# A two-block transformer kernel on one core: prepared weights, conditioning rows and normed inputs are given out to the engines at other places

## The chip, the core and the metric

The kernel runs on one core of a Trainium2 chip. The core has a matrix engine (PE, which also loads weights: PEld), a vector engine (DVE), an activation engine (ACT), a general engine (POOL) and SyncE (SP), whose queue issues the DMAs. Each engine takes its own instructions strictly in program order and waits for others through semaphores. The metric is the device time of one execution in microseconds, less is better. A difference of 0.2% (about 4 us) is what repeated measurements of this kernel can tell from none.

## The reference

There are 1024 tokens of width 1024, in fp32. A first block mixes (a short and a 31-tap convolution) and has a gated FFN; a second part has one layer with a causal mean pool and one of sliding-window attention, both conditioned by a vector `c`. Cut to what the change touches:

```
g = dwconv(h @ w_gate, conv_ffn_w);  v = h @ w_up
x = x + (silu(g) * v) @ w_down

shift, scale, gate = split(silu(c) @ ada_w[l] + ada_b[l], 3)     # l = 0, 1; the same for kv_ada
h = rmsnorm(rmsnorm(x, norm_final_g), norm_g[0]) * (1 + scale) + shift
u, z = split(h @ a_w_in, 2)
y = (grouped(pool(u), a_w_group) * a_scale * silu(z)) @ a_w_out
x = x + gate * y
k, v = split((rmsnorm(x) * kv_norm_g ... + shift_kv) @ w_kv)
x = x + gate * (attention(h1, k, v) * silu(z)) @ b_w_out;  return rmsnorm(x)
```

## The kernel before, in words

Activations lie transposed, 128 features by 512 tokens in a tile (`c` = 0 or 1 is the half of the tokens). Each fp32 operand is cut in two parts of a shorter format, `hi` (a copy, on ACT) and `lo` (the difference, on POOL or DVE), and each product is three matmuls of 512 columns: hi*hi, lo*hi, hi*lo. The order of every engine's work is the order of the calls in the source (`manual_schedule`); nothing is moved by a planner.

The stages, by time in the profiled execution: input projection and convolutions (0 to 250 us), `w_out` (255 to 344), FFN gate and up products (344 to 776), `w_down` (776 to 1040), the pooled layer's input products (1040 to 1379), its grouped products and output (1379 to 1658), keys and values (1658 to 1690), attention (1690 to 1975), the end (to 2058).

**Products by pairs.** FFN and pooled input products are done for pairs of weight columns and pairs of token halves by seven products instead of eight (class `Pair`, `Products.run`). One step is one product: 12 matmuls. Four of the seven need sums or differences of raw weight halves (`ws`, made by DVE). For each step `prep_to` makes the weights of the step `PREP_AHEAD` = 4 later in one call: `added` on DVE (`ws`), `ACT.copy` to `whi`, and `wlo` on POOL, or on DVE for two of seven. `lead` does the same during the rows of `w_out`, by a table.

**Chains.** Work beside the products is written as generators. `pump` steps each of them once, once per row or step (twice in part of the FFN), and takes a piece from the queue `bg`. `ada_all` is such a chain: for 64 row blocks of the conditioning weights it loads a tile `adaw` (128x1024, 512 KB) and adds it, times a scalar, to two accumulators on DVE, 8 blocks to each of 8 sections, and then sums over partitions. `chain_pool` makes the normed input of the pooled layer from the column sums of squares: `bsum` on DVE, `sums` on PE, a power on POOL, a diagonal on DVE and ACT (`dh`, `dl`), `spread` on PE, then scaled blocks. At its end it makes `R1` by another `diag(power(m))` and `spread`. `WAIT` and bare `yield`s set how many steps lie between these parts.

**Buffers.** `S` takes one of `NS` = 92 slots of 128x512 in turn, `L` one of 8 wide tiles (128x1060) for the convolution's tiles, `adaw`, and in the pooled layer `up` and the running sums `ps`. A tile that takes a used slot waits until its last reader is done, a store to memory (`pp<-ps`) being a reader.

**Pooled output.** `load_group` loads the pooled rows of a group (`pl`) and splits them (`cut`: `ahi` on ACT, `alo` on POOL). `do_gm(g, todo)` does a group's products, each followed by `sz` (DVE) and its split, and takes four pieces of `todo` per row; for the first group `todo` holds loads and 16 times `scale_x` (DVE). `out2` does the output products. `attn` chains then make the normed input (`make_h`: `hu`, `hlo` on DVE); `finish` runs a chain to its end at once.

Of the kernel before, what the change touches and what calls it, by code (L numbers as in the profile page):

```python
# [30 lines left out]
        "ffn0": (2, 1, 1), "ffn1": (4, 1, 3), "pool0": (2, 1, 1), "pool1": (5, 1, 3),  # L31
# [32 lines left out]
def kernel(ctx: ExitStack, tc: tile.TileContext, a: dict, out: bass.AP):  # L64
# [3 lines left out]
    NS = 92  # L68
# [8 lines left out]
    wide = wide_ctx.enter_context(tc.tile_pool(name="wide", bufs=8))  # L77
# [760 lines left out]
    class Pair:  # L838
# [12 lines left out]
        def keep(self, x):  # L851
            hi, lo = S("whi", F32R), S("wlo", F32R)
            ACT.copy(hi, x)  # L853
            small_op["n"] += 1
            eng = DVE if not small_op["early"] and small_op["n"] % 7 in SUB_DVE else POOL
            eng.tensor_tensor(lo, x, r32(hi), ALU.subtract)  # L856
            return hi, lo

# [13 lines left out]
        def prep(self, p):  # L872
# [17 lines left out]
            self.w[p] = self.keep(t)  # L890
# [111 lines left out]
    class Products:  # L1002


        def __init__(self, stage, put):
            self.pairs, self.steps = stage
            self.group = {g: Pair(*g, put(*g)) for g in self.pairs}
            self.ready = 0

        def prep_to(self, n):  # L1010
            while self.ready < min(n, len(self.steps)):
                g, p = self.steps[self.ready]
                self.group[g].prep(p)
                self.ready += 1

        def lead(self, row):

            small_op["early"] = True
            n = row - SUMS_FROM
            if 0 <= n < 2 * SIDE:  # L1020
# [27 lines left out]
    for c in range(NC):  # L1048
        finish(ln[c])
        acc = S("ss")  # L1050
        for d in range(NK):
# [6 lines left out]
            sq_into(acc, x, d == 0)  # L1058
# [12 lines left out]
    def ada_section(i):  # L1071
        kind, l, s = sections[i]
        h = {}
        halves = (slice(0, CH), slice(CH, D))

        def one(k):
            t = L("adaw")
            src = a["ada_w_2"][l] if kind == "ada" else a["kv_ada_w_2"]
            nc.sync.dma_start(out=t[:, 0:D], in_=src[k * 128:(k + 1) * 128, s * D:(s + 1) * D])
            h[k] = t  # L1080

        def mac(k):
            t = h.pop(k)
            if k == 0:
                h["acc"] = P("ada"), P("ada")
            for n, hs in enumerate(halves):
                src = h["acc"][n]
                if k == 0:
                    DVE.tensor_scalar(src, t[:, hs], cact[:, 0:1], None, ALU.mult)
                    continue  # L1090
                dst = src
                if k == 7:
                    dst = h["sum", n] = S("adas")
# [932 lines left out]
```

## Time and profile before

| | |
|---|---|
| median of 3 executions | 2061.04 us (2061.02 to 2062.11) |
| profiled execution | 2060.43 us |
| its span in the trace | 2058.7 us |
| mean granted PE clock | 0.982 |
| PE busy | 1960.1 us (95%) |
| DVE / ACT / POOL busy | 1498.2 / 840.2 / 1011.3 us |

The span goes from the first to the last instruction of the trace; 1.7 us of the execution lie around it. PE matmuls are pipelined, so their busy times overlap; an engine's waits are the idle time before an instruction, with the instruction that released it.

### The profile page before, as it was taken

What the parts mean: (1) busy time and instruction counts of PE and PEld (TensorE: products, weight loads), DVE (VectorE), ACT (ScalarE), POOL (GpSimd) and SP (SyncE); (2) the same over time, 40 slices, a digit from 0 to 9 for tenths busy, and PEclk for the clock granted to TensorE, in tenths of its full rate; (3) what the DMA queues carried; (4) which work ended last, traced back from release to release, by engine and by line L of the source; (5) the groups of instructions that cost most, each with busy time, mean ns of one, the idle gap of its engine ahead of it and who ended that gap; (6) DMA issues with size and microseconds to landing.
All of it is one profiled execution on the core that took longest, in us unless ns stands there. A gap on an engine that the chain in (4) does not pass through costs nothing. (4 is left out here: it accounts for less than half of the span.)

```text
span 2058.7 us, 26114 instructions
## 1 busy us (share of the span) xinstructions
PE 1960.1 (95%) x8920; PEld 1620.7 (79%) x8920; DVE 1498.2 (73%) x2339; ACT 840.2 (41%) x1647; POOL 1011.3 (49%) x851
## 2 busy tenths in 40 slices
PE   7999998999999999999889999988999989999997
PEld 6888876787877878888667788866888778888886
DVE  7899778889978986343776766758444687787866
ACT  6333344433333343211355233233213357778723
POOL 4767465754534468642456343365426353224422
PEclk9999999999999999999989999999999999999999
DMA  6111412045989468532201343256332032111302
GB/s 211 52 62 41 144 62 72 8 143 169 179 156 187 143 217 306 198 122 78 77 31 42 123 129 102 87 208 237 123 120 76 11 123 65 54 57 32 113 1 82
DMA packets 116709, 228.61 MB, mean 111 GB/s; under 512 B 13232, under 2 KB 19808, under 8 KB 116576
## 3 DMA queue, kind: packets, MB, share of 16 engines
q1 hardware_dynamic: 116576, 226.95, 34.9%
q8 instruction: 70, 1.15, 0.2%
q14 instruction: 63, 0.52, 0.1%
HBM read 177.62 MB, written 48.23 MB: 110 GB/s over the span
## 5 line engine op out<-in xcount | busy, mean ns | idle before, releaser
L903 PE MATMUL p<-hhi,whi 128*128 128x512 f32 x1064 | 420.3, 395 | 19.4 <-ACT p L912 11.0
L903 PE MATMUL p<-hhi,wlo 128*128 128x512 f32 x1064 | 418.1, 393 | 8.5 <-POOL wlo L856 8.0
L903 PE MATMUL p<-hlo,whi 128*128 128x512 f32 x1064 | 417.4, 392 | 0.0
L195 POOL TENSOR_TENSOR wlo<-raw,whi 128x512 fp32r<-128x512 f32 x196 | 260.3, 1352 | 183.8 <-ACT whi L194 113.1
L310 PE MATMUL p<-ahi,whi 128*128 128x512 f32 x784 | 312.0, 398 | 5.4 <-DVE sz L1433 3.2
L310 PE MATMUL p<-alo,whi 128*128 128x512 f32 x784 | 310.7, 396 | 1.5 <-POOL alo L421 1.3
L310 PE MATMUL p<-ahi,wlo 128*128 128x512 f32 x784 | 310.3, 396 | 0.0
L856 POOL TENSOR_TENSOR wlo<-ws,whi 128x512 fp32r<-128x512 f32 x116 | 166.7, 1440 | 250.0 <-ACT whi L853 215.7
L903 PEld LDWEIGHTS p<-hhi,whi 128*128 128x128 f32 x1064 | 201.7, 190 | 66.6 <-ACT p L912 13.7
L903 PEld LDWEIGHTS p<-hhi,wlo 128*128 128x128 f32 x1064 | 201.8, 190 | 54.5 <-POOL wlo L856 11.1
L903 PEld LDWEIGHTS p<-hlo,whi 128*128 128x128 f32 x1064 | 202.1, 190 | 41.7
L853 ACT CAST whi<-ws 128x512 fp32r<-128x512 f32 x152 | 92.8, 620 | 270.7 <-DVE ws L861 253.3
L301 PE MATMUL p<-hhi,whi 128*128 128x512 f32 x496 | 196.1, 395 | 6.6 <-ACT hhi L414 6.6
L301 PE MATMUL p<-hlo,whi 128*128 128x512 f32 x496 | 195.6, 394 | 3.3 <-DVE hlo L415 3.3
L301 PE MATMUL p<-hhi,wlo 128*128 128x512 f32 x496 | 195.0, 393 | 0.0
L310 PEld LDWEIGHTS p<-ahi,whi 128*128 128x128 f32 x784 | 150.4, 192 | 38.7 <-DVE sz L1433 4.1
L856 POOL TENSOR_TENSOR wlo<-raw,whi 128x512 fp32r<-128x512 f32 x84 | 120.5, 1440 | 117.8 <-ACT whi L853 109.0
L310 PEld LDWEIGHTS p<-alo,whi 128*128 128x128 f32 x784 | 150.6, 192 | 33.7 <-POOL alo L421 1.6
L310 PEld LDWEIGHTS p<-ahi,wlo 128*128 128x128 f32 x784 | 150.3, 192 | 31.8
L194 ACT CAST whi<-raw 128x512 fp32r<-128x512 f32 x196 | 112.1, 617 | 113.7 <-PE p L310 75.8
L528 DVE SCALAR_TENSOR_TENSOR cps<-u,vec,cps 128x1024 f32<-128x1024 f32 (+1 forms) x140 | 150.6, 1075 | 4.5
L1439 DVE SCALAR_TENSOR_TENSOR x<-p,modv,x 128x512 f32<-128x512 f32 x128 | 94.6, 749 | 67.2 <-PE p L310 66.8
(288 smaller groups left out, 3709.8 us busy)
## 6 DMA issues: line engine op xcount, KB each, us to landing
adaw<-in_ada_w SPq DMA_DIRECT2D x48, 512.0 KB, 6.1
raw<-in_a_w_in SPq DMA_DIRECT2D x64, 256.0 KB, 4.2
raw<-in_w_gate SPq DMA_DIRECT2D x44, 256.0 KB, 5.3
raw<-in_w_up SPq DMA_DIRECT2D x44, 256.0 KB, 6.0
ff<-f SPq DMA_DIRECT2D x44, 256.0 KB, 2.8
raw<-in_w_down SPq DMA_DIRECT2D x44, 256.0 KB, 5.1
fl<-ff SPq DMA_DIRECT2D x44, 256.0 KB, 5.4
raw<-in_w_in SPq DMA_DIRECT2D x40, 256.0 KB, 3.1
```

The source lines that it names most:

```text
L194: (DVE.tensor_copy if on_dve else ACT.copy)(hi, t)
L195: (DVE if on_dve else POOL).tensor_tensor(lo, t, r32(hi), ALU.subtract)
L301: PE.matmul(ps, lhsT=wt[k // 4][:, sl], rhs=hh[k, c], start=(n == 0), stop=(n == 23))
L310: PE.matmul(ps, lhsT=wt[d // 4][:, sl], rhs=hh[c], start=(n == 0), stop=(n == last))
L528: DVE.scalar_tensor_tensor(dst[:, lo:hi], u[:, lo + k:hi + k], V("conv_b_w", k * 4 + j), src[:, lo:hi], ALU.mult, ALU.add)
L853: ACT.copy(hi, x)
L856: eng.tensor_tensor(lo, x, r32(hi), ALU.subtract)
L903: PE.matmul(ps, lhsT=wt[:, sl], rhs=hh, start=(begins and n == 0), stop=(n == 11), skip_group_check=True)
L1439: DVE.scalar_tensor_tensor(X[d, c], ps, modv[:, goff + d:goff + d + 1], X[d, c], ALU.mult, ALU.add)
```

## The change

- `prep_to` gives the weights out in three calls: at a step, the `lo` on DVE of the product prepared a call before, then `whi` and the POOL `lo`, and last the source (`ws` or the raw half) of the product after it. `PREP_AHEAD` is 5. The table of `lead` and the rows in which sums are made are new.
- `ada_all` loads the conditioning rows in two halves of 256 KB into general slots, two row blocks ahead across sections; it starts 6 steps later; a section's last sums are a chain of their own. `NS` is 96, and there are 6 wide tiles instead of 8; the pool `qp` of attention's `qa`, `qb` is gone (they take slots).
- The squares of the first half of `w_out` are added on POOL.
- `sums` of the pooled input's first half comes one row later; `R1` 24 and 8 `yield`s later instead of 1 and 3.
- The first group's cuts come one at a step, from one step earlier on, the odd ones on DVE. `do_gm(0)` takes two pieces of `todo` per row and splits `sz` on POOL; half of `scale_x` is left to `out2`.
- In attention's first chain 4 `yield`s come before `make_h`, and the chain is run to its end after the key and value products, not ahead of them.

```
-        "ffn0": (2, 1, 1), ... "pool0": (2, 1, 1), ...
+        "ffn0": (2, 1, 1), ... "pool0": (3, 1, 1), ...
-PREP_AHEAD = 4
-FFN_DMA = 120
-LEAD = (2, 4, 5, 6, 6, 6, 7, 8)
-SUMS_FROM = 3
+PREP_AHEAD = 5
+FFN_DMA = 126
+LEAD = (3, 5, 6, 6, 7, 7, 8, 8)
+SUMS_ROWS = (0, 1, 2, 3, 4, 5, 6, 11)
+ADA_AHEAD = 2
-    NS = 92
+    NS = 96
-    wide = wide_ctx.enter_context(tc.tile_pool(name="wide", bufs=8))
+    wide = wide_ctx.enter_context(tc.tile_pool(name="wide", bufs=6))
...
         def prep_to(self, n):
+            for f in [self.queue.pop(0) for _ in range(len(self.queue))]:
+                f()
             while self.ready < min(n, len(self.steps)):
                 g, p = self.steps[self.ready]
-                self.group[g].prep(p)
+                self.queue.append(lambda p=p, pair=self.group[g], x=self.group[g].source(p): self.high(pair, p, x))
                 self.ready += 1
+        def high(self, pair, p, x):
+            hi, lo = S("whi", F32R), S("wlo", F32R)
+            ACT.copy(hi, x)
+            pair.w[p] = hi, lo
+            small_op["n"] += 1
+            if small_op["early"] or small_op["n"] % 7 not in SUB_DVE:
+                POOL.tensor_tensor(lo, x, r32(hi), ALU.subtract)
+            else:
+                self.queue.append(lambda: DVE.tensor_tensor(lo, x, r32(hi), ALU.subtract))
...
-            sq_into(acc, x, d == 0)
+            sq_into(acc, x, d == 0, None, POOL if c == 0 else None)
...
+    def ada_load(n):
+        ...
+        for h in range(2):
+            t = S("adaw")
+            nc.sync.dma_start(out=t, in_=src[k * 128:(k + 1) * 128, s * D + h * CH:s * D + (h + 1) * CH])
+            ada_w[n].append(t)
...
     def ada_all():
-        for i in range(8):
-            yield from ada_section(i)
+        for n in range(ADA_AHEAD):
+            ada_load(n)
+            yield
+        for n in range(8 * len(sections)):
+            ada_load(n + ADA_AHEAD)
+            for _ in range(ADA_GAP):
+                yield
+            ...
+            yield
+            if k == 7:
+                launch(ada_fin(n // 8, h))
...
-        if n == 2 * EARLY + 5 * SIDE:
+        if n == 2 * EARLY + 5 * SIDE + 6:
             chains.append(ada_all())
...
         yield from blocks_of_h(c, get, shift)
-        yield
+        for _ in range(24):
+            yield
         d1 = diag(power(m), POOL)
-        for _ in range(3):
+        for _ in range(8):
             yield
...
-            PP_H[g, k, c], PP_L[g, k, c] = split(tiles.pop((k, c)))
+            PP_H[g, k, c], PP_L[g, k, c] = split(tiles.pop((k, c)), DVE if g == 0 and k % 2 else None)
...
-                    put_act(("m", i), c, split(t, DVE if c else None))
-                    for _ in range(min(4, len(todo))):
+                    put_act(("m", i), c, split(t, DVE if c and g else None))
+                    for _ in range(min(per, len(todo))):
...
-        if left <= 8:
-            for f in nxt["cut"][:2]:
+        if left <= 9:
+            for f in nxt["cut"][:1]:
...
-    do_gm(0, todo)
+    do_gm(0, todo, 2)
     for g in range(3):
         todo = [f for part_ in load_group(g + 1) for f in part_]
-        out2(g, 0, todo, 2 if g == 2 else 1)
+        if g == 0:
+            todo = scales[8:] + todo
+        out2(g, 0, todo, 1 if g == 1 else 2)
...
-        yield
+        for _ in range(4 if c == 0 else 1):
+            yield
         yield from make_h(c, t, 8, MOD_SH1, *SPREAD[f"attn{c}"])
...
-    finish(pend[0])
     for c in range(NC):
         ...
         vt[c] = evac_v(c, kvps[1, c])
+    finish(pend[0])
     finish(pend[1])
```

Where the instructions now stand is told at three places. The first is DVE in the FFN, a few steps of one pair (`ws` a weight sum, `wlo` a low part, `c`, `f` and `g` the gate's convolution and the products' sums). Before:

```order
L968 TENSOR_TENSOR g<-p,p_4396 128x512
L856 TENSOR_TENSOR wlo<-raw,whi 128x512
L942 SCALAR_TENSOR_TENSOR c_4650<-g,vec,c_4650 128x1024
L996 TENSOR_TENSOR f<-p,p_4421 128x512
L861 TENSOR_TENSOR ws<-raw 128x512
L861 TENSOR_TENSOR ws<-ws,raw 128x512
L942 SCALAR_TENSOR_TENSOR c_4650<-g,vec,c_4650 128x1024
L968 TENSOR_TENSOR g<-p,q 128x512
L861 TENSOR_TENSOR ws<-raw 128x512
L861 TENSOR_TENSOR ws<-ws,raw 128x512
L856 TENSOR_TENSOR wlo<-ws,whi 128x512
```

And now:

```order
L990 TENSOR_TENSOR f<-p,p_4431 128x512
L1021 TENSOR_TENSOR wlo<-raw,whi 128x512
L854 TENSOR_TENSOR ws<-raw 128x512
L854 TENSOR_TENSOR ws<-ws,raw 128x512
L936 SCALAR_TENSOR_TENSOR c_4667<-g,vec,c_4667 128x1024
L962 TENSOR_TENSOR g<-p,q 128x512
L1131 SCALAR_TENSOR_TENSOR ada<-adaw,cact,ada 128x512 x2
L978 TENSOR_TENSOR f<-f,c_4667 128x512
L990 TENSOR_TENSOR f<-p,q 128x512
L1021 TENSOR_TENSOR wlo<-ws,whi 128x512
L936 SCALAR_TENSOR_TENSOR c_4722<-g,vec,c_4722 128x1024
```

The two weight sums stand at the same place among the products' sums or one ahead, and the `wlo` of a sum, which followed it at once, now has a step's other work ahead of it, half a block of conditioning among it.

The second place is POOL near the end of the pooled input products, where the pooled rows of the first group are cut (`alo<-pl`) between the weights (`wlo`). Before:

```order
L856 TENSOR_TENSOR wlo<-ws,whi 128x512
L421 TENSOR_TENSOR alo<-pl,ahi 128x512 x2
L856 TENSOR_TENSOR wlo<-raw,whi 128x512
L421 TENSOR_TENSOR alo<-pl,ahi 128x512 x2
L856 TENSOR_TENSOR wlo<-ws,whi 128x512
L195 TENSOR_TENSOR wlo<-raw,whi 128x512 x2
L1340 MEMSET up 128x16
L421 TENSOR_TENSOR alo<-pl,ahi 128x512 x2
L856 TENSOR_TENSOR wlo<-ws,whi 128x512
```

And now:

```order
L1019 TENSOR_TENSOR wlo<-ws,whi 128x512
L422 TENSOR_TENSOR alo<-pl,ahi 128x512
L1019 TENSOR_TENSOR wlo<-raw,whi 128x512
L422 TENSOR_TENSOR alo<-pl,ahi 128x512
L1019 TENSOR_TENSOR wlo<-ws,whi 128x512
L196 TENSOR_TENSOR wlo<-raw,whi 128x512 x2
L1355 MEMSET up 128x16
L1019 TENSOR_TENSOR wlo<-ws,whi 128x512
L422 TENSOR_TENSOR alo<-pl,ahi 128x512
```

Between two weights there stands one cut where there were two, and the last `wlo` shown has no cut between it and the pair of group weights ahead of it.

The third place is DVE where the pooled block ends (`hu`, `hlo` of the attention's input, half 0; `tr`, `bsum` the column sums of the squares of half 1; `r` what follows from them). Before:

```order
L1285 SCALAR_TENSOR_TENSOR hu<-x,gain,R 128x512
L1279 SCALAR_TENSOR_TENSOR hlo<-hu,modv,hhi 128x512
L1285 SCALAR_TENSOR_TENSOR hu<-x,gain,R 128x512
L1279 SCALAR_TENSOR_TENSOR hlo<-hu,modv,hhi 128x512
L1525 COPY kvb<-sums 32x1 x4
L1439 SCALAR_TENSOR_TENSOR x<-p,modv,x 128x512
L415 SCALAR_TENSOR_TENSOR hlo<-x,gain,hhi 128x512 x2
L338 STREAM_TRANSPOSE tr<-ssa 128x512
L339 TENSOR_REDUCE bsum<-tr 128x16
L361 TENSOR_SCALAR r<-sums 32x4 x4
L371 CAST rh<-q 128x4
L372 TENSOR_TENSOR rl<-q,rh 128x4
```

And now:

```order
L416 SCALAR_TENSOR_TENSOR hlo<-x,gain,hhi 128x512 x2
L339 STREAM_TRANSPOSE tr<-ssa 128x512
L340 TENSOR_REDUCE bsum<-tr 128x16
L1299 SCALAR_TENSOR_TENSOR hu<-x,gain,R 128x512 x2
L1293 SCALAR_TENSOR_TENSOR hlo<-hu,modv,hhi 128x512
L1299 SCALAR_TENSOR_TENSOR hu<-x,gain,R 128x512
L1293 SCALAR_TENSOR_TENSOR hlo<-hu,modv,hhi 128x512
L1299 SCALAR_TENSOR_TENSOR hu<-x,gain,R 128x512 x2
L1293 SCALAR_TENSOR_TENSOR hlo<-hu,modv,hhi 128x512
L1299 SCALAR_TENSOR_TENSOR hu<-x,gain,R 128x512
L1293 SCALAR_TENSOR_TENSOR hlo<-hu,modv,hhi 128x512
L362 TENSOR_SCALAR r<-sums 32x4 x4
```

The column sums, which stood behind all `hu` and `hlo` of half 0, now stand ahead of ten of these instructions, and `r` stands behind them.

## Rows read from the trace of the kernel before

**Rows 1.** Busy time, share and instructions of each engine, from the profile page.

```profile
PE 1960.1 (95%) x8920; PEld 1620.7 (79%) x8920; DVE 1498.2 (73%) x2339; ACT 840.2 (41%) x1647; POOL 1011.3 (49%) x851
```

**Rows 2.** Waits of PE, whole span: line, releaser, us in total, times, longest.

```profile
PE sums L346 <- DVE bsum L339: 18.8, 5, 6.9
PE spread L382 <- DVE dh L374: 17.0, 5, 7.8
PE p L903 <- ACT p L912: 11.0, 6, 3.2
PE p L903 <- POOL wlo L856: 8.0, 5, 4.2
...
PE p L903 <- DVE q L915: 5.8, 2, 4.9
```

**Rows 3.** Stretches: length, busy us (instructions) by engine, clock, DMA, GB/s.

```profile
250.00:344.00 94.00, 82.85 (x341) 66.21 (x340) 79.14 (x118) 46.22 (x88) 62.73 (x48) 0.95 0.23 79
500.00:640.00 140.00, 133.06 (x578) 107.44 (x577) 117.82 (x154) 48.59 (x75) 60.43 (x56) 1.00 0.81 165
640.00:776.00 136.00, 131.31 (x573) 107.31 (x572) 118.09 (x153) 53.10 (x86) 77.19 (x68) 0.99 0.61 188
776.00:1009.00 233.00, 233.00 (x1032) 192.99 (x1031) 111.18 (x164) 58.56 (x97) 117.99 (x92) 1.00 0.47 162
1009.00:1083.00 74.00, 54.34 (x207) 42.44 (x205) 55.93 (x86) 38.11 (x71) 43.46 (x38) 0.86 0.10 36
1083.00:1160.00 77.00, 72.09 (x301) 58.99 (x302) 55.40 (x70) 33.76 (x60) 43.89 (x35) 0.94 0.27 92
1340.00:1380.00 40.00, 34.55 (x138) 26.31 (x137) 18.71 (x22) 16.17 (x30) 30.19 (x25) 0.96 0.73 251
1380.00:1420.00 40.00, 33.82 (x131) 26.01 (x130) 36.88 (x45) 8.85 (x16) 13.70 (x16) 0.92 0.67 244
1626.00:1690.00 64.00, 53.50 (x223) 43.11 (x222) 53.65 (x85) 31.51 (x56) 35.59 (x25) 0.92 0.26 93
```

**Rows 4.** Waits of all engines between 344 and 776 us.

```profile
ACT whi L853 <- DVE ws L861: 159.7, 43, 12.8
...
DVE ada L1089 <- DMA adaw<-in_kv_ada_w: 10.6, 2, 8.5
...
DVE wlo L856 <- ACT whi L853: 9.3, 13, 0.8
```

**Rows 5.** DVE around the first pooled products: start, us, operation, idle before.

```profile
1050.93 0.69 DVE L339 TENSOR_REDUCE bsum<-tr 128x16 f32<-128x512 f32 x1
1052.63 0.69 DVE L374 TENSOR_TENSOR dh<-ident,rh 128x512 fp32r<-128x512 f32 x1 [1.01 <-POOL rh L371]
```

**Rows 6.** DVE at the stall near 1150 us.

```profile
1154.57 1.28 DVE L915 TENSOR_TENSOR q<-p,p 128x512 f32<-128x512 f32 x2
```

**Rows 7.** POOL at the stall near 1371 us.

```profile
1370.58 3.47 POOL L421 TENSOR_TENSOR alo<-pl,ahi 128x512 fp32r<-128x512 f32 x2
1374.02 1.25 POOL L856 TENSOR_TENSOR wlo<-ws,whi 128x512 fp32r<-128x512 f32 x1
```

**Rows 8.** DVE at the first grouped products.

```profile
1402.27 3.08 DVE L1450 SCALAR_TENSOR_TENSOR x<-x,vec,R 128x512 f32<-128x512 f32 x3
```

**Rows 9.** DVE between the pooled block and attention.

```profile
1675.68 0.69 DVE L339 TENSOR_REDUCE bsum<-tr 128x16 f32<-128x512 f32 x1
...
1681.15 0.69 DVE L374 TENSOR_TENSOR dh<-ident,rh 128x512 fp32r<-128x512 f32 x1
```

**Rows 10.** DVE operations by form: count, busy us, mean ns, idle before.

```profile
L856 DVE TENSOR_TENSOR wlo<-ws,whi 128x512 fp32r<-128x512 f32 x36 | 38.6, 1072 | 19.2 <-ACT whi L853 18.6 <-POOL wlo L856 0.5
...
L915 DVE TENSOR_TENSOR q<-p,p 128x512 f32<-128x512 f32 x38 | 25.7, 681 | 5.2 <-PE p L903 5.1
```

**Rows 11.** DMA issues by line: count, KB each, median us to landing.

```profile
adaw<-in_ada_w SPq DMA_DIRECT2D x48, 512.0 KB, 6.1
...
pp<-ps SPq DMA_DIRECT2D x16, 512.0 KB, 2.9
```

More of the change, by code (lines that the diff above doesn't have):

```diff
@@ L849, in half @@
             return self.raw[u][h]
[L851 to L857, printed above, removed]
         def added(self, x, y, op):
@@ L1069, with ada_fin, ada_all @@
                 + [("ada", 1, s) for s in range(3)])
-    def ada_section(i):
-        kind, l, s = sections[i]
-        h = {}
[L1074 to L1083, printed above, removed]
+    ada_w = {}
+    halves = (slice(0, CH), slice(CH, D))
+    def ada_load(n):
+        if n >= 8 * len(sections):
+            return
+        kind, l, s = sections[n // 8]
+        k = n % 8
+        src = a["ada_w_2"][l] if kind == "ada" else a["kv_ada_w_2"]
+        ada_w[n] = []
+        for h in range(2):
+            t = S("adaw")
+            nc.sync.dma_start(out=t, in_=src[k * 128:(k + 1) * 128, s * D + h * CH:s * D + (h + 1) * CH])
+            ada_w[n].append(t)
+    def ada_fin(i, h):
+        kind, l, s = sections[i]
+        y = small.tile([128, 32], F32, tag="bsum", name="bsum", bufs=3)
+        for n in range(2):
+            block_sums(h["sum", n], CH, y[:, 16 * n:16 * n + 16])
+            yield
+        for _ in range(10):
+            yield
+        b = VEC_OFF["ada_b_2"] + l * 24 + s * 8 if kind == "ada" else VEC_OFF["kv_ada_b_2"] + s * 8
+        ps = quad_sums(y)
+        for n in range(4):
+            q = slice(32 * n, 32 * n + 32)
+            DVE.tensor_tensor(modv[q, i * 8:(i + 1) * 8], ps[q, n:32:4], vec[q, b:b + 8], ALU.add)
+        ada_done.append(i)
+    ada_done = []
+    def ada_all():
+        for n in range(ADA_AHEAD):
+            ada_load(n)
+            yield
+        h = {}
+        for n in range(8 * len(sections)):
+            k = n % 8
+            ada_load(n + ADA_AHEAD)
+            for _ in range(ADA_GAP):
+                yield
+            ts = ada_w.pop(n)
             if k == 0:
-                h["acc"] = P("ada"), P("ada")
-            for n, hs in enumerate(halves):
-                src = h["acc"][n]
+                h = {"acc": (P("ada"), P("ada"))}
+            for m in range(2):
+                src = h["acc"][m]
                 if k == 0:
-                    DVE.tensor_scalar(src, t[:, hs], cact[:, 0:1], None, ALU.mult)
+                    DVE.tensor_scalar(src, ts[m], cact[:, 0:1], None, ALU.mult)
                     continue
@@ L1092, in mac @@
                 if k == 7:
[L1093 to L1116 removed]
+                    dst = h["sum", m] = S("adas")
+                DVE.scalar_tensor_tensor(dst, ts[m], cact[:, k:k + 1], src, ALU.mult, ALU.add)
             yield
[L1118 to L1122 removed]
+            if k == 7:
+                launch(ada_fin(n // 8, h))
+        while len(ada_done) < len(sections):
+            yield
         for o, sc, g in ((0, 1, VEC_OFF["norm_g_2"]), (8, 6, VEC_OFF["norm_g_2"] + 8),
@@ L1414, in load_group, with do_gm @@
                 [lambda k=k, c=c: cut(k, c) for k, c in kc])
-    def do_gm(g, todo):
+    def do_gm(g, todo, per=4):
         for hh in range(2):
```

50 lines of the change are left out of this document (13 added, 37 removed).

## The prediction

> **What bounds the kernel now.** I read the page's busy times first: PE is busy 95% of the span, DVE 73% as a mean [rows 1]. So the time is PE's work plus what PE loses, and the mean of DVE says little: what counts is where DVE, ACT or POOL are late for PE. That is in the waits of PE [rows 2]: column sums (18.8 us), the spread that follows from them (17.0), evacuations on ACT and DVE (11.0 and 5.8), low parts of weights (8.0). The view by stretches then tells where, with the clock [rows 3]. One stretch, 776 to 1009, has no loss: 1032 matmuls in 233.0 us are 0.226 us for one, 2.71 for a step of 12. I take each other stretch's length less its matmuls times 0.226 as its loss. This counts waits and the slower clock in one (a granted clock under 1.00 means that part of the stretch ran at 1.2 instead of 2.4 GHz, after PE had waited):
>
> 250 to 344 loses 17.0 us; 500 to 640 and 640 to 776 lose 9.4 and 6.5, the FFN thus 15.9; 1009 to 1083 loses 27.2; 1083 to 1160, 9.0; 1340 to 1380, 8.8; 1380 to 1420, 10.4; 1626 to 1690, 13.6 [rows 3]. Together 102 us, and each part of the change touches one of these. It removes no matmul, so 102 us is the ceiling, and the question is what of each loss goes and what comes in its place.
>
> **The FFN (15.9 us).** ACT sat 159.7 us in 43 waits for DVE's `ws` before a `whi`, and DVE in turn 9.3 us for ACT before a `wlo` [rows 4]: source, high and low part of one weight are called together, so each engine's next work stands behind the other's. In the new order of DVE the sum is out a step before it is wanted and the `wlo` a step after, which takes both waits away. ACT's waits cost PE only where the copies of `p` behind them are late; part of the 11.0 us is that [rows 2]. The conditioning rows kept DVE waiting 10.6 us in two waits, the longer 8.5 [rows 4]: at 512 KB a tile lands 6.1 us after its issue at the median [rows 11], and it is asked for 4 to 6 pumps, some 5 to 8 us, ahead (3 `yield`s and the row before; two pumps a step of 2.71 us). Now it is asked for 11 pumps ahead, some 15 us. DVE's work doesn't shrink: it is busy 235.9 of these 276 us, 85% [rows 3], and with the loss gone it would be 91%. At that load queues stay, so I take 7 us of the 15.9 back. Bounds: 14 back (all but what stands behind ACT's evacuations), or 5 lost if the 64 tiles' halves, now sharing slots with raw weights on one in-order issue queue whose DMA engines are 81% busy [rows 3], arrive later than before.
>
> **w_out (17.0 us).** The sums of half 1 aren't moved. Seven additions of squares go from DVE to POOL, which is busy 62.7 of 94 us [rows 3]; they free DVE and delay POOL's. I take 1 us, bounds -3 and +3 (the wait for `bsum` here is one of five in 18.8 us, 3.8 on average [rows 2]).
>
> **Entry to the pooled products (27.2 us).** `sums` of half 0 one row later takes 2.7 us off the wait before it, which at the mean is 3.8 [rows 2]. `R1` of half 0 held PE 7.8 us, the longest wait of its kind [rows 2]: its `dh` began at 1052.63 and PE had been there at 1045.6. What was late was not `R1` alone: POOL and DVE were still at the squares of half 1, whose `bsum` ended at 1051.6 [rows 5]. In the new order PE goes past the place of `R1`, and 6 matmuls on (1.4 us) meets the `sums` of half 1. It would be there at about 1044.5 (1045.6, plus 1.4, less the 2.7 gained). One row's evacuation fewer lies between (about 2 us of DVE), so that `bsum` ends near 1050: a new wait of some 5 us in the place of 7.8. Before, those sums ran at 1057.9, behind the spread and at the slower clock, so at that point the gain is near 8 us; 2 of them I give back for the slower clock that a 5 us wait will again bring (granted 0.86 here, the lowest of all stretches [rows 3]). I take 6, bounds 2 (the squares are as late as now and the spread after them too) and 10.
>
> **The wait of 4.9 us near 1150 (9.0 us with the clock).** PE waited for `q` [rows 2], which DVE began at 1154.57 [rows 6] behind running sums, weight sums and a `wlo` that waits for ACT. The last of these, about 1.9 us with its wait, is out of its way. I take 4.5, bounds 0 (the running sums alone made it late) and 8.
>
> **Cuts and weights (8.8 us).** At 1370.58 POOL made two cuts, 3.47 us, and only then the `wlo` that PE waited 4.2 us for [rows 2, 7]. In the new order no cut stands before it and half of the cuts are DVE's, which is busy 18.7 of these 40 us [rows 3]. I take 7: the 3.5 of the cuts at least, all 8.8 at most.
>
> **First grouped products (10.4 us).** DVE is busy 36.9 of 40 us [rows 3]: four pieces of `todo` a row are up to four `scale_x` of 1.03 us (three took 3.08 [rows 8]) against a row of 2.71. Two pieces a row, 2.1 us, and no `alo` fit into it. The other eight `scale_x` come under `out2`, whose rows are shorter, and make DVE late for a few of them, but PE has the rest of its eight accumulators to go on with. I take 8.5, bounds 4 and 10.4.
>
> **Keys and values (13.6 us).** PE waited 6.9 us for the `bsum` of half 1 [rows 2], which ended at 1676.4 behind `hu` and `hlo` [rows 9]; PE was there at 1669.5. Ten of these go behind it; at 1.1 us each (the mean of a `wlo`, of the same size, in [rows 10]) `bsum` ends 11 us earlier, near 1665, and the wait is gone. But `r` stands behind the ten: `dh` will end as before, at 1681.8 [rows 9], and PE, with 37 matmuls (8.4 us) between, is there at 1677.9. So 3.9 of the 6.9 come back as a wait for the spread. With 1 us of clock I take 4, bounds 2.5 and 7.
>
> **New waits.** 96 slots serve more kinds of tiles, and the wide tiles are six. I take 2 us, bounds 0 and 8 (one wait like the 8.5 of [rows 4], moved on to PE).
>
> **The sum.** 7 + 1 + 6 + 4.5 + 7 + 8.5 + 4 - 2 = 36 us. The profiled execution took 2060.4 us (span 2058.7 and 1.7 around it), 0.6 under the median, so 2024.4 there and **2025** for the median.
>
> **A rule that speaks against it.** A `wlo` on DVE, which reads two operands from SBUF, takes 1072 ns, and a `q` of the same size, which reads one from PSUM, 681 [rows 10]; so 0.4 us of a DVE instruction passes in a wait that no idle time shows. The Trainium skill (SBUF — State Buffer, "SBUF: two separate sides") says that DVE and GpSimd share a pair of SBUF ports by an exclusive lock, and that a DVE operation with two SBUF inputs and a GpSimd operation block each other for a whole instruction. The row agrees in its sign. In the FFN the work on both engines stays and is packed closer, so the waits that the three calls remove could return as longer instructions: the FFN's 7 us would be nought, 2032. It is the first rival.
>
> **Rivals.**
> - DVE is the bound of the FFN. For it: 85% busy now, the longer two-operand instructions [rows 3, 10]. Against: 8.5 us of its waits were for one tile that came late. Time: 2032, and down to 2037 if the loads get later by the 5 us above. Chance 0.17.
> - The waits move instead of going: at the entry and at keys and values I find the successor already (5 and 3.9 us). If the same holds near 1150 and in the first grouped products, where DVE's total work stays, 4.5 and 8.5 fall to nothing, and the FFN gives 3 instead of 7: a gain of 19, 2042. Chance 0.18.
> - No change to be told: the places where PE waits are set by DVE's total work, which is the same; gain under 4 us, 2057 to 2065. Against: the cuts' and the `bsum`'s waits are of order, as the rows show. Chance 0.05.
> - Slower: the six wide tiles. A running sum takes a wide tile whose last reader may be a store, which lands 2.9 us after its issue [rows 11]. There are 16 such stores. If each held DVE for the whole 2.9 us and DVE, already the late engine near 1150, handed it on, it would be 46 us, and 36 - 46 is 10 us slower, 2071. It decides from 2.3 us a store on (36 / 16). Against: DVE has 21.6 of 77 us free in that stretch [rows 3], and a tile is reused only after five others. Chance 0.07.
> - More than forecast, every upper bound but the FFN's: 2005. Chance 0.07.
> - The forecast itself, 2012 to 2036: 0.46.
>
> Faster by over 0.2% (4 us, what a measurement of this kernel tells from none) are all but the third and fourth: 0.88; same 0.05; slower 0.07. From 2007 to 2047 no more than 2 in 10 is left out.
>
> **What would show it.** Right: ACT's idle time before `whi` for `ws` falls to a fraction of 159.7 us in the FFN; DVE has no wait of several us for `adaw`; no PE wait for `wlo` near 1371 and none for `sz` behind; a PE wait of about 5 us for `bsum` of half 1 in place of the 7.8 us for `R1`; a wait of about 4 us for the spread in place of the 6.9 for `bsum` before attention. Wrong: `ps` on DVE waiting for a store, SP waiting for slots in the FFN with PE waiting for `wlo` or `whi` of a late raw half, or DVE's mean for two-operand instructions rising by the time that its waits fell.

## The result, and the profile after

The changed kernel takes 2037.53 us (median of 4 runs, 2036.70 to 2041.84) where the kernel before takes 2061.57 beside it (2061.02 to 2063.30). The ratio is 0.9886, with a 95% interval of 0.9869 to 0.9903: 24.0 us less. I had predicted 2025.0, within 2007 to 2047.

The profiled execution's span is 2034.9 us, 23.8 less than before. The busy times of the page:

```profile
PE 1948.4 (96%) x8920; PEld 1616.6 (79%) x8920; DVE 1507.3 (74%) x2332; ACT 839.0 (41%) x1647; POOL 1026.5 (50%) x858
```

Against [rows 1] PE executes the same 8920 matmuls in 12 us less of busy time: fewer of them run at the slower clock (mean granted clock 0.984, before 0.982). The waits of PE over the whole span (line, releaser, us in total, times, longest):

```profile
PE sums L347 <- DVE bsum L340: 19.8, 6, 5.2
PE spread L383 <- DVE dh L375: 18.2, 4, 7.5
...
PE p L897 <- ACT p L906: 5.4, 3, 2.6
...
PE p L897 <- DVE u L912: 3.7, 1, 3.7
PE p L1442 <- DVE alo L422: 3.1, 1, 3.1
...
PE p L897 <- POOL wlo L1019: 1.1, 1, 1.1
PE p L897 <- DVE q L909: 0.9, 2, 0.5
```

Against [rows 2], the waits for evacuations, for `wlo` and for `q` shrank from 24.8 to 7.4 us. Those for column sums and for the spread did not: 38.0 us now, 35.8 before. Two waits of a single place are larger or new: for `u` (3.7 us, where the kernel before has one of 1.8) and for a cut of the first group at the grouped products (3.1).

The stretches (length, busy us and instructions by engine, clock, DMA share, GB/s):

```profile
344.00:380.00 36.00, 29.16 (x120) 23.37 (x119) 28.31 (x35) 16.34 (x33) 19.88 (x20) 0.91 0.04 16
500.00:640.00 140.00, 139.56 (x616) 114.40 (x615) 124.54 (x173) 51.87 (x81) 64.22 (x60) 1.00 0.83 173
640.00:776.00 136.00, 129.53 (x559) 105.47 (x558) 121.29 (x162) 52.51 (x85) 74.09 (x65) 0.97 0.71 213
1009.00:1083.00 74.00, 58.21 (x235) 46.52 (x234) 52.60 (x79) 42.78 (x77) 48.94 (x41) 0.88 0.10 36
1083.00:1160.00 77.00, 75.59 (x334) 62.27 (x333) 58.82 (x80) 30.10 (x57) 42.56 (x36) 1.00 0.27 96
1380.00:1420.00 40.00, 38.45 (x170) 31.52 (x169) 35.13 (x41) 14.04 (x25) 36.29 (x25) 1.00 0.66 240
```

By the measure of [rows 3] (matmuls times 0.226 us), 500 to 640 lost 9.4 us and loses 0.8 now; 1009 to 1083 went from 27.2 to 20.9, 1083 to 1160 from 9.0 to 1.5, and 1380 to 1420 from 10.4 to 1.6. But 640 to 776 rose from 6.5 to 9.7, and the 36 us from 344 on lose 8.9, where they lost 1.9. Their row before:

```profile
344.00:380.00 36.00, 34.11 (x151) 27.93 (x150) 30.09 (x35) 17.58 (x36) 22.90 (x21) 1.00 0.04 15
```

Since the stages have shifted against each other, I also take the time at which PE starts the same matmul, counted in program order (the two matmuls of a column sum, `sums`, as one), in both traces. The difference between two places is what the part between them gained:

```
place (matmul)                    before     after   after-before   part gains
start of w_out's 2nd half (1150)   283.3     283.1       -0.1
FFN, 35 steps in (1425)            357.4     361.8       +4.4      w_out   -4.4
FFN (2400)                         582.8     585.7       +2.9
FFN (2600)                         634.7     631.1       -3.6
FFN (2700)                         661.4     660.8       -0.5
end of the FFN (3130)              762.9     761.0       -1.9      FFN      6.3
w_down (4200)                     1007.4    1005.0       -2.4
pooled products begun (4500)      1104.9    1094.6      -10.4      entry    8.0
after the stall of 1150 (4800)    1180.9    1164.3      -16.6      1150     6.3
end of pooled products (5640)     1380.3    1356.2      -24.0
first grouped product (5720)      1398.4    1380.8      -17.6      cuts     1.0
output of group 0 (5850)          1438.8    1412.1      -26.7      grouped  9.1
before keys and values (6835)     1668.0    1641.3      -26.7
attention begun (6950)            1702.4    1676.3      -26.0      k, v    -0.7
attention, 2nd half (8300)        1939.3    1915.7      -23.7      attn.   -2.3
```

The last column, with 0.5 between 3130 and 4200 (it lies at the FFN's last waits, before 3160), adds up to 23.8. Gains at the same place, by the same code, vary between executions, mostly by 1 to 2 us; at the entry the nine experiments that leave its code alone gain 5.0 to 8.9 us. That the slower clock lasts longer or shorter after a stall is a likely reason, not a shown one. Below, a difference of medians under some 4 us counts only where the trace shows it at the place itself. The end of a trace is below matmul 8800, ahead of the closing norm; behind it executions differ by up to another 2 us.

### The profile page after: what moved, and what is told of

Its sections match the earlier page's. It is cut to its first block, busy times and chain, and to the rows that moved or that the text cites. A ratio compares the mean times of both kernels' runs of the same rounds, so it can differ in the third digit from the quotient of the medians.

```text
span 2034.9 us, 26328 instructions
## 1 busy us (share of the span) xinstructions
PE 1948.4 (96%) x8920; PEld 1616.6 (79%) x8920; DVE 1507.3 (74%) x2332; ACT 839.0 (41%) x1647; POOL 1026.5 (50%) x858
## 2 busy tenths in 40 slices
DMA packets 125926, 228.63 MB, mean 112 GB/s; under 512 B 14256, under 2 KB 20832, under 8 KB 125792
## 5 line engine op out<-in xcount | busy, mean ns | idle before, releaser
L196 POOL TENSOR_TENSOR wlo<-raw,whi 128x512 fp32r<-128x512 f32 x196 | 264.0, 1369 | 181.8 <-ACT whi L195 129.3
L1019 POOL TENSOR_TENSOR wlo<-raw,whi 128x512 fp32r<-128x512 f32 x84 | 123.5, 1477 | 105.4 <-ACT whi L1015 75.1
```

The costliest lines, as they stand in the source:

```text
L196: (DVE if on_dve else POOL).tensor_tensor(lo, t, r32(hi), ALU.subtract)
L1019: POOL.tensor_tensor(lo, x, r32(hi), ALU.subtract)
```

## The experiments

All twelve kernels were timed in five rounds beside the kernel before (its medians 2061.94 to 2062.17). "After" is the changed kernel.

**1. The squares back on DVE.**

```
-            sq_into(acc, x, d == 0, None, POOL if c == 0 else None)
+            sq_into(acc, x, d == 0)
```

> The changed kernel with one part undone: the squares of the first half of w_out are added on DVE again. In the changed kernel PE is 4.4 us behind the kernel before at the FFN's first products, with a new wait of 5.1 us for the second half's column sums. Theory: the additions on POOL delay the first half's sums or lengthen DVE's two-operand instructions, and that wait shrinks by at least 3 us, the total to about 2034. Rival: PE is only there earlier (the spread ahead of it no longer waits) and the new table of weight sums sets DVE's time; then the wait stays at 4 to 6 us and the total at 2037, or above by the 2 us of DVE that POOL had taken over.

2037.82 us, ratio 0.9882 (0.9869 to 0.9896). The wait of 5.1 us for `bsum` at the start of the FFN stays; PE is there 0.5 us earlier, at its end 0.6 later than in after. The squares on POOL are worth nothing and are not what costs `w_out` 4.4 us.

**2. The odd cuts back on POOL.**

```
-            ... = split(tiles.pop((k, c)), DVE if g == 0 and k % 2 else None)
+            ... = split(tiles.pop((k, c)))
```

> The changed kernel with all cuts of the first group on POOL again, still one at a step. In the changed kernel the gain of 7.4 us up to the last pooled products is given back by a wait of 3.1 us of PE for a cut on DVE and 3.4 us of slower clock. Theory: DVE makes that cut late since it stands behind the running sums, which wait for POOL's zeroing; on POOL it is out in time, the wait goes and the total falls by about 6 us to 2031. Rival: four more cuts of 1.3 to 1.7 us keep POOL behind, a wlo comes late by some 4 us as in the kernel before, and the total stays within 2 us of 2037 or goes to 2040.

2042.29 us, 0.9902 (0.9888 to 0.9915). The cut on DVE that PE waited 3.1 us for is gone, but not the stall; PE's waits between 1330 and 1385:

```profile
PE p L1442 <- POOL ps L1374: 4.5, 2, 3.7
PE p L1442 <- ACT ahi L421: 1.2, 1, 1.2
```

From there to the first output products PE loses 2.7 us more than in after; 1.7 us of the rest lie in `w_out`, where the kernels are the same. So the half of the cuts on DVE is no loss by itself. The first row names a `memset` of the running sums' edge (`ps`), but POOL's timeline shows that PE waits for a cut here too:

```profile
1363.79 3.48 POOL L196 TENSOR_TENSOR wlo<-raw,whi 128x512 fp32r<-128x512 f32 x2
1367.23 1.25 POOL L422 TENSOR_TENSOR alo<-pl,ahi 128x512 fp32r<-128x512 f32 x1
```

PE goes on at 1368.54, when this cut is done (1368.48); it stood behind two `wlo` of group weights. Further back in the same chain DVE's running sums wait 6.2 us for a `memset` that POOL does in its order; experiment 8 takes that up.

**3. Attention's first chain as before.**

```
-        for _ in range(4 if c == 0 else 1):
+        for _ in range(1 if c == 0 else 1):
...
+    finish(pend[0])
     for c in range(NC):
...
-    finish(pend[0])
     finish(pend[1])
```

> The changed kernel with the normed input of attention put back: one yield, and the first chain run to its end ahead of the key and value products. In the traces this part changed nothing (0.6 us later at the first attention products): 6.9 us of waiting for the column sums became 7.0 us for the spread. Theory: the total stays at 2036 to 2039, with 7 us for the sums and none for the spread. Rival, my prediction's size: it is worth 4 us and the total goes to 2041.

2042.08 us, 0.9901 (0.9888 to 0.9915). Between matmul 6835 and the first attention products (6900) PE takes 0.04 us less than in after: by the trace the new order gains nothing there, though the median, 4.5 us over after, would by itself fit the rival of 2041. PE waits 6.9 us for `bsum`, where after waits 7.0 for the spread. Of the 6.0 us by which PE is later at the end of this execution, 3.9 are there by the end of the pooled entry (4500) and 1.6 come just before 8300, where this kernel's code is that of after; I count them as variation.

**4. Eight steps ahead of half 0's `make_h` instead of four.**

```
-        for _ in range(4 if c == 0 else 1):
+        for _ in range(8 if c == 0 else 1):
```

> The changed kernel with 8 instead of 4 yields before the first attention chain's normed input, so that its ten instructions on DVE, and the two cuts on POOL, stand behind the second half's inverse root instead of ahead of it. Theory: the spread's 7.0 us of wait fall below 3 us, total about 2032. Rival: the normed input of half 0 is then late for the first attention products, and the 5 us come back there: 2037, or more.

2039.49 us, 0.9897 (0.9883 to 0.9912). PE reaches the first attention products 9.8 us earlier, and gives 5.9 and 1.9 us back right behind them; among the whole kernel's waits of PE there is a new one:

```profile
PE vT L1599 <- ACT vt L1593: 4.8, 1, 4.8
```

Half 1's `make_h` now meets the value products' evacuations. The 9.8 us were there to be had, but not by moving half 0 alone.

**5. `R1` as before.**

```
-        ... "pool0": (3, 1, 1), ...
+        ... "pool0": (2, 1, 1), ...
-        for _ in range(24):
-            yield
+        yield
         d1 = diag(power(m), POOL)
-        for _ in range(8):
+        for _ in range(3):
```

> The changed kernel with the entry to the pooled products put back: the first half's sums a row earlier, R1 one and three yields behind the blocks. In the traces this stretch gave 8.6 us where I had forecast 6. Theory: undone it costs 6 to 9 us, total about 2045, with a wait of some 8 us for R1's spread. Rival: the stretch gained because DVE and ACT were ahead by the three calls; then a wait of under 4 us for R1 comes back and the total is at 2039.

2046.90 us, 0.9927 (0.9915 to 0.9940). PE's timeline at the first pooled products, and its longest wait there:

```profile
1052.30 0.79 PE L383 MATMUL spread<-dh,ones 128*128 128x512 f32 x1 [10.81 <-DVE dh L375]
```

From the end of `w_down` to 4500 it gains 1.3 us on the kernel before, after 8.0. So the place of `R1`, with the row by which `sums` comes later, makes most of the entry's gain; which of the two, this run doesn't tell apart.

**6. The weights given out in one call**, with the tables of before (`prep_to`, `LEAD`, `SUMS_FROM`, `PREP_AHEAD` 4, `FFN_DMA` 120).

```
-                self.queue.append(lambda p=p, pair=..., x=...source(p): self.high(pair, p, x))
+                self.group[g].prep(p)
-LEAD = (3, 5, 6, 6, 7, 7, 8, 8)
-SUMS_ROWS = (0, 1, 2, 3, 4, 5, 6, 11)
+LEAD = (2, 4, 5, 6, 6, 6, 7, 8)
+SUMS_FROM = 3
```

> The changed kernel with the weights of pairs made in one call again, 4 steps ahead, with the tables of the kernel before. Theory: the FFN's gain (6.3 us in the traces) and that near 1150 us (6.2) come from the three calls, so the total goes up by 8 to 12 us to about 2047, and the waits for q near 1140 and for u, q and p in the FFN come back; the loss of 4.4 us at w_out may go. Rival, the conditioning rows gave the FFN's part: then only the 6 us near 1150 come back, 2043, or less.

2046.02 us, 0.9921 (0.9907 to 0.9935), 8.5 over after, of which its trace shows 6.1. All engines' waits between 344 and 776, the two rows that the three calls were to remove:

```profile
ACT whi L854 <- DVE ws L862: 143.6, 50, 7.3
...
DVE wlo L857 <- ACT whi L854: 12.4, 11, 4.1
```

They are nearly those of [rows 4], and yet the FFN gains 6.4 us on the kernel before, as much as with three calls (6.3); by matmul 3160, behind the stage's last waits, it is 5.5 against 6.8. `w_out` doesn't lose the 4 us. What is lost against after comes later: 1.3 us by 3160, 2.7 at the pooled entry (within what executions differ by there), 3.8 around 1150, where PE waits 3.6 us for `q`, 0.9 before 5600 and 1.5 at the cuts.

**7. The conditioning rows as before**: tiles of 512 KB in 8 wide tiles, `NS` 92, `qa` and `qb` in their own pool; the three calls stay.

```
-            t = S("adaw")
+            w = L("adaw")
...
-    NS = 96
+    NS = 92
-    ... tc.tile_pool(name="wide", bufs=6))
+    ... tc.tile_pool(name="wide", bufs=8))
-        qa, qb = S("qa", F32R), S("qb", F32R)
+        qa = qp.tile([128, CH], F32R, tag="Q", name="qa")
+        qb = qp.tile([128, CH], F32R, tag="Q", name="qb")
```

> The changed kernel with the conditioning rows as before (512 KB into wide tiles, one ahead within a section, 92 slots, 8 wide tiles, a pool of its own for qa and qb). Theory: the wait of some 8 us of DVE for a row comes back and the FFN loses 3 to 5 us, total about 2041. Rival: rows two ahead were worth nothing, since the FFN of the changed kernel still stops for u by 3.7 us; the total stays within 2 us of 2037; and if six wide tiles cost in the pooled stage, it falls under 2036.

2052.41 us, 0.9950 (0.9938 to 0.9963). The FFN loses 8.6 us against the kernel before, 14.9 against after. Waits of all engines between 344 and 776:

```profile
DVE ada L1096 <- DMA adaw<-in_kv_ada_w: 11.7, 2, 8.2
...
PE p L897 <- DVE wlo L1021: 10.5, 5, 4.4
```

Attention doesn't lose its 2.3 us here: PE waits 1.7 us in two for `prob` between 1870 and 1960, 4.0 in three in after.

**8. The running sums' edge cleared on DVE.**

```
-                POOL.memset(n[:, 0:16], 0.0)
+                DVE.memset(n[:, 0:16], 0.0)
```

> The changed kernel, and the zeroing of the first 16 columns of each running sum is done by DVE instead of POOL. The second run of cuts has shown that POOL can't take the cuts either. Theory: what is late near 1360 us is DVE's chain of running sums, which waits 2.5 and 1.5 us for POOL's zeroing behind weights; without it the cut on DVE is 4 us earlier, PE's wait of 3.1 us and the slow clock behind it go, total 2031 to 2033. Rival: DVE has too much work there (sums, cuts, evacuations) and the wait stays over 2 us, total 2036 to 2038.

2039.88 us, 0.9895 (0.9880 to 0.9910). PE's waits between 1330 and 1420:

```profile
PE p L311 <- DVE x L1454: 4.5, 3, 1.7
...
PE p L1442 <- DVE alo L422: 0.9, 1, 0.9
```

The wait for the cut falls from 3.1 to 0.9 and PE gains 5.3 us up to 5720, but loses 3.7 at the output products behind and 1.6 later. 0.2 us are left: PE now waits for evacuations (`x`) that stand on DVE behind two `scale_x` each.

**9. Both halves' `make_h` later.**

```
-        for _ in range(4 if c == 0 else 1):
+        for _ in range(8 if c == 0 else 6):
```

> The changed kernel with 8 yields before the normed input of half 0 and 6 before that of half 1 (4 and 1). With 8 and 1 the wait of 7.0 us for the spread was gone and PE was 9.8 us ahead at the first attention products, and 7.8 of it went again: the evacuation of the values of half 1 stood on DVE and ACT behind the normed input of half 1, and PE waited 4.8 us for it. Theory: with both behind the evacuations the 6 to 8 us stay, total 2030 to 2032. Rival: the normed input of half 1 is then itself late for attention, and the gain goes there as well: 2036 to 2038.

2031.55 us, 0.9849 (0.9831 to 0.9867), 6.0 under after. PE's waits between 1590 and 1690:

```profile
PE sums L347 <- DVE bsum L340: 2.4, 1, 2.4
PE spread L383 <- DVE dh L375: 1.2, 1, 1.2
```

The wait of 7.0 us is gone, PE is at the first attention products 9.8 us earlier, and 8.0 stay to the end (7.2 in the whole span).

**10. The last weight sums of `w_out` in row 9 instead of 11.**

```
-SUMS_ROWS = (0, 1, 2, 3, 4, 5, 6, 11)
+SUMS_ROWS = (0, 1, 2, 3, 4, 5, 6, 9)
```

> The changed kernel with the last of the weight sums made in row 9 of w_out instead of row 11. The runs showed that the squares on POOL are not what made the second half's column sums late (5.1 us with them on DVE as well), and that the old tables of the one-call form lost 3.9 us less there. Theory: the two sums of row 11 stand on DVE ahead of the second half's squares, at 1.7 us each, while DVE sits idle by 5.2 us around row 9; moved there, the wait falls from 5.1 to 2 us or less and the total by 3 to 6 us to about 2033. Rival: the wait is there because PE comes earlier than before, and DVE's blocks of h set the end of the sums; then it stays at 4 us or more and the total within 2 us of 2037.

2035.35 us, 0.9864 (0.9842 to 0.9886). PE's waits between 330 and 380: for `bsum` 1.1 us instead of 5.1.

```profile
PE sums L347 <- DVE bsum L340: 1.1, 1, 1.1
```

PE is at matmul 1425 6.0 us earlier. By the end of this execution 1.0 is left (1.1 lost in the FFN, 2.9 at the pooled entry, 1.5 before keys and values, 0.6 gained there), and this execution as a whole is 0.4 us longer than after's; so its own time doesn't tell it from after, the place does.

**11. The bias rows' DMAs in the pooled products instead of the FFN.**

```
     def in_ffn(n, left):
-        if n == 50:
-            bias_load()
-        if n == 60:
-            bias_rows()
-        if n > 60 and n % 3 == 0 and bias_out:
-            bias_out.popleft()()
...
     def in_pooled(n, left):
+        if n == 10:
+            bias_load()
+        if n == 20:
+            bias_rows()
+        if n > 20 and n % 3 == 0 and bias_out:
+            bias_out.popleft()()
```

> The changed kernel with the position bias (16 small-packet DMAs of 192 KB) written in the pooled products instead of the FFN. In the changed kernel DVE stops 6.8 and 2.5 us in the FFN for a slot whose last reader is a store ff<-f, and PE 3.7 us for u behind it, with the clock after it. Theory: the bias DMAs hold the 16 DMA engines so that stores land late and slots come free late; without them the wait for u goes and the total falls 5 to 8 us to about 2031. Rival: the store is late because its issue stands on the in-order queue behind loads that wait for slots; then DVE's wait stays over 4 us and the total within 2 us of 2037.

2037.07 us, 0.9879 (0.9861 to 0.9897). The wait for `u` and DVE's waits for stores of `f` are gone and the FFN gains 7.1 us between 2600 and 2700. Between 4500 and 4800 it loses 6.1; PE's wait there:

```profile
PE p L897 <- ACT whi L1015: 4.2, 1, 4.2
```

So those DMAs are the cause of the stall in the FFN. That they cost as much at the new place isn't shown: no engine waits for a DMA between 1083 and 1170. DVE works there from 1114 to 1138 without a gap, so that weight sums, and ACT's `whi` from them, are late for a PE that comes 7.1 us earlier than in after.

**12. The edits of 8 to 11 together.**

> The changed kernel with four edits at once: DVE zeroes the running sums, weight sums in row 9, the bias in the pooled products, 8 and 6 yields in attention's chains. Theory: the edits are at four places of the program with full PE stretches between, so their gains add: about 6 (attention), 4 (w_out), 6 (FFN) and 0 to 2, total 2020 to 2024. Rival: what is gained at one place is a wait at the next, as with the zeroing alone, and the total is over 2030.

2024.99 us (2021.32 to 2025.81), 0.9816 (0.9797 to 0.9835): 12.5 under after and 37 under the kernel before, the fastest of all, and just over the 2020 to 2024 expected of gains that add. Its largest waits of PE are the same two, smaller:

```profile
PE sums L347 <- DVE bsum L340: 13.8, 6, 4.4
PE spread L383 <- DVE dh L375: 11.3, 3, 7.5
```

Of the 12.3 us in its trace 6.0 come in the second half of `w_out` and 9.8 at keys and values; of the 7.1 that the moved bias rows bring in the FFN, 6.0 go again near 1150. The four alone left 10.3 in theirs.

## Why the prediction was right and where it failed

The direction and the mechanism were right: PE's losses shrink at the places named. Of the 36 us only 23.8 came, so that the time lies in the range, but 1.5 us above the forecast's own (2012 to 2036). Three terms failed; they make up 16 us of shortfall, the others together came out 4 us better. (One bound was added up wrong: the upper bounds of "more than forecast" make 54 us, 2007 and not 2005.)

```
term                    forecast   measured
FFN                        7          6.3
w_out                      1         -4.4
entry, pooled              6          8.0
stall near 1150            4.5        6.3
cuts and weights           7          1.0
first grouped products     8.5        9.1
keys and values            4         -0.7
new waits                 -2         -2.3 (attention); the FFN's are in its term
```

**The FFN: right size, in part for the wrong reason.** ACT's wait for `ws` fell by half:

```profile
POOL wlo L1019 <- ACT whi L1015: 113.9, 39, 10.8
...
ACT whi L1015 <- DVE ws L854: 72.7, 28, 11.5
...
DVE tr L339 <- DMA ff<-f: 6.8, 1, 6.8
```

But in experiment 6, where it stays at 143.6, the FFN gains nearly as much. That wait cost PE 1.3 us at most; so the agreement of 6.3 with the forecast 7 is in part luck. Of the 87 us that this wait of ACT's shrank against the kernel before, 57 came back in its waits for DVE's `c` and `g` (48.2 us before, 105.1 now). The 6.5 us that both gain between 2400 and 2600, and that experiment 7 doesn't, come from the conditioning rows (their size, lead and slots together), and there the step was right. Before, DVE waited for them twice in that stretch:

```profile
609.63 1.41 DVE L1089 TENSOR_SCALAR ada<-adaw,cact 128x512 f32<-128x512 f32 x2 [8.46 <-DMA adaw<-in_kv_ada_w]
...
618.23 1.41 DVE L1094 SCALAR_TENSOR_TENSOR ada<-adaw,cact,ada 128x512 f32<-128x512 f32 x2 [2.70 <-DMA adaw<-in_kv_ada_w]
```

All of DVE's waits for `adaw`, 21.1 us in ten (the 10.6 of the prediction are one line's), are 2.3 in two now. The two parts hang together, which I had not seen: the three calls put DVE's `wlo` a step nearer to its use, behind the row that DVE waits for, so that with late rows PE waits for it (10.5 us in experiment 7). The rows gain 6.4 us without the three calls and 14.9 with them. The three calls' own gain, after against experiment 6, is 6.2 us in the pooled products (3.8 of the 6.3 around 1150, and 2.4 behind) and up to 4.0 between (1.3 by 3160, 2.7 at the entry), and they cost 3.9 at `w_out`. What part of these is the tables' and what the calls', no run here tells apart.

The last row of the first fence above is the rival's mechanism of a tile whose last reader is a store, in a slot where I had put it in a wide tile: DVE waits 6.8 us for a store of `f`, `u` comes late and PE waits 3.7, at the slower clock behind it (0.97 in 640 to 776). Experiment 11 shows what makes the store late. No wait of PE's shows a cost of the six wide tiles.

**`w_out`: the step that failed.** "The sums of half 1 aren't moved" looked at the column sums alone. DVE's timeline shows what I didn't price, the weight sums that the new table puts into row 11:

```profile
333.81 1.77 DVE L854 TENSOR_TENSOR ws<-raw 128x512 f32<-128x512 f32 x1
335.50 1.77 DVE L854 TENSOR_TENSOR ws<-raw,ws 128x512 f32<-128x512 f32 x1
...
350.19 0.71 DVE L339 STREAM_TRANSPOSE tr<-ss 128x512 f32<-128x512 f32 x1
350.93 0.69 DVE L340 TENSOR_REDUCE bsum<-tr 128x16 f32<-128x512 f32 x1
```

They stand ahead of the last squares, 3.5 us, and from there to `bsum` DVE has no idle time, so that they go into PE's wait whole (5.1). Against the kernel before only part of them is new. It made two such sums in row 10, also behind `dh` and ahead of the last squares:

```profile
330.83 0.69 DVE L861 TENSOR_TENSOR ws<-raw 128x512 f32<-128x512 f32 x1
331.43 0.68 DVE L861 TENSOR_TENSOR ws<-raw,ws 128x512 f32<-128x512 f32 x1
```

They took 1.4 us, the same work in row 11 takes 3.5. Beside them POOL stood idle, and it works beside those of row 11; before, then after:

```profile
332.20 1.29 POOL L856 TENSOR_TENSOR wlo<-raw,whi 128x512 fp32r<-128x512 f32 x1 [2.42 <-ACT whi L853]
```

```profile
333.30 3.43 POOL L737 TENSOR_TENSOR hlo<-h,hhi 128x512 fp32r<-128x512 f32 x2
```

So `bsum` ends 2.5 us later than before (351.6, 349.1), and PE, which had waited 2.0 us for the spread ahead and doesn't now, is there 2.8 us earlier (346.6, 349.4). PE then runs for some us at the slower clock (0.91 in 344 to 380). Experiment 10 moves these two and takes 4.0 us of the wait and 2.0 behind it away.

**The entry: right, and moved as foreseen.** PE meets the `bsum` of half 1 with 5.2 us of wait ("some 5"). It wasn't foreseen that the first spread's wait grows from 3.5 to 7.5 as the `sums` ahead of it no longer wait for 4.1: PE came earlier, but `dh` didn't. I had counted a wait that comes back at the next link of its chain at two places; it held here and at the cuts too, and for more at keys and values.

**Near 1150: right.** No wait for `q` over 0.5 us is left.

**Cuts: gain given back.** The `wlo` near 1371 isn't waited for, as predicted, and PE is 7.4 us ahead at 5640. Then it waits for a cut. POOL and DVE there:

```profile
1355.34 1.22 DVE L1375 TENSOR_TENSOR ps<-ps 128x1024 f32<-128x1024 f32 x1 [2.48 <-POOL ps L1374]
...
1359.80 2.28 DVE L1375 TENSOR_TENSOR ps<-ps 128x1024 f32<-128x1024 f32 x1 [1.50 <-POOL ps L1374]
...
1362.60 1.15 DVE L422 TENSOR_TENSOR alo<-pl,ahi 128x512 fp32r<-128x512 f32 x1
```

```profile
1351.74 3.52 POOL L196 TENSOR_TENSOR wlo<-raw,whi 128x512 fp32r<-128x512 f32 x2
1355.19 0.15 POOL L1374 MEMSET ps<- 128x16 f32 x2
```

A cut that DVE does stands behind running sums, these wait for a `memset` of 0.15 us, and that waits in POOL's order behind two `wlo` of group weights, 3.52 us. (The second wait, of 1.50, ends with a `memset` behind a cut of POOL's that had waited 3.1 us for ACT.) I had asked only what the cuts delay on POOL, not what they now stand behind on DVE. Experiment 8 shows the link: with the `memset` on DVE the wait falls to 0.9.

**Grouped products: right,** and the eight `scale_x` left to the output products cost 1.5 us of PE's waits, as foreseen, though each takes far longer there (below).

**Keys and values: the wait moved whole.** The wait for `bsum` went, and PE waits 7.0 us for the spread where I had 3.9. DVE and POOL ahead of it:

```profile
1651.47 0.67 DVE L362 TENSOR_SCALAR r<-sums 32x4 f32<-32x4 f32 x4
1657.20 0.17 DVE L372 CAST rh<-q 128x4 fp32r<-128x4 f32 x1 [5.07 <-POOL q L390]
```

```profile
1652.48 1.26 POOL L422 TENSOR_TENSOR alo<-hu,ahi 128x512 fp32r<-128x512 f32 x1 [3.48 <-ACT ahi L421]
1653.71 2.48 POOL L196 TENSOR_TENSOR wlo<-raw,whi 128x512 fp32r<-128x512 f32 x2
1656.15 1.02 POOL L390 TENSOR_TENSOR q<-r,neghalf 128x4 f32<-128x4 f32 x1
```

I had put `r` behind the ten moved instructions, and it is; but the power `q` on POOL stands behind a cut that waited for ACT, and two `wlo`, 3 to 4 us that I didn't count. Before, PE came to this spread after its slower stretch, with `dh` long done; now the slower clock lies behind the wait. Experiment 9, in which only three of the ten stand ahead of `r`, takes the wait away.

**Attention.** 2.3 us are lost where the change only has `qa` and `qb` take slots. Experiment 7, with the pool back, doesn't lose them, but undoes other things too; that the slots are the cause is likely and not shown.

**The rivals.** That DVE is the FFN's bound fell: the FFN gave 6.3. The longer two-operand instructions that it was built on came elsewhere, at `w_out` and in `scale_x` (below). "The waits move instead of going" (2042) was nearer to the time than the forecast, but at other places than it named: 1150 and the grouped products held, `w_out`, the cuts and keys and values did not.

## What to carry to other kernels

A wait that an engine off the critical path shows is no sum to win back: the three calls took 71 us of ACT's waits for `ws` away (143.6 to 72.7) and PE gained 1.3 us at most in that stage, while two waits of DVE for conditioning rows, 11.2 us, were worth 6.5 to PE. When an instruction is moved, follow the whole chain to the next thing that PE waits for, through every engine's order (`r` on DVE, then `q` on POOL, then `dh`; a 0.15 us `memset` behind 3.5 us of `wlo`), and price what stands ahead at each link. A table that moves fillers by a row or two (`SUMS_ROWS`) can cost as much as a main edit brings: two rows earlier, two sums took 4.0 us off a wait of 5.1 (experiment 10).

## What the runs showed of the hardware

A DVE instruction with two operands from SBUF lengthens where POOL is busy. `scale_x`, the same 16 instructions (ns min, median, max), after and, in the second fence, before:

```profile
L1465 DVE SCALAR_TENSOR_TENSOR x<-x,vec,R x16: 734/1227/1792, 1373.2 to 1399.1; 128x512 f32<-128x512 f32 x16
```

```profile
L1450 DVE SCALAR_TENSOR_TENSOR x<-x,vec,R x16: 734/746/1779, 1396.2 to 1415.7; 128x512 f32<-128x512 f32 x16
```

POOL is busy 36.3 of 40 us there now, 13.7 before [rows 3]. The Trainium skill (SBUF — State Buffer, "SBUF: two separate sides") has a DVE operation with two SBUF inputs and a GpSimd operation that reads SBUF lock each other out of a shared port pair for whole instructions; these rows agree in sign, and so do the two weight sums of `w_out`, 0.69 and 0.68 us beside an idle POOL and 1.77 each beside its `hlo`. By that rule I had feared for the FFN, where it did not bite anew: there the sums, `wlo` and convolution pieces on DVE (`ws`, `wlo`, `c`) take 169.4 us in all by the groups of both traces, though `c` alone rose from 1451 to 1594 ns.

PE's clock is lower behind a wait (granted 0.88 in 1009 to 1083, with waits of 7.5 and 5.2 us), and a matmul shows it directly: the spread that followed the wait of 7.0 us took 0.80 us, the one at the pooled entry without a wait 0.39.

Stores of `f` land 4.2 us after their issue at the median where they took 2.8 before, with more and smaller transfers beside them (125,926 packets for the 228.6 MB of the run, 116,709 before); the bias rows' transfers of 192 KB take 9.3. With these moved out of the FFN (experiment 11) the stores take 2.3. A DVE instruction whose slot was last read by such a store waited up to 6.8 us.
